# Group 0's scores at a later place, and the weighed probabilities of groups 1 and 2 turned by DVE and memory instead of TensorE

## The chip, the cores and the metric

The kernel runs on one core of a Trainium2 chip, as one launch. The metric is the device time of one execution in microseconds, and the profile is of one execution on the chip. Engines are named as the profile names them: PE is TensorE, DVE VectorE, ACT ScalarE, POOL GpSimd, SP the queue that loads weights; PEld is TensorE's loading of the stationary operand.

## What is computed

Two layers of a decoder over 512 tokens of width 1024, each a mixer and a gated MLP with a convolution of width 3. The change lies in the mixer of the second layer: three groups of dilated causal attention, four heads of width 128 each. Cut to what matters:

```python
DIL_PATTERNS = ((128, 1), (512, 4), (2048, 16))        # window, dilation

def odd_mixer(h, w_in, q_gain, k_gain, w_out):
    z = (h @ w_in).reshape(B, S, DIL_GROUPS, 3, DIL_HEADS, DIL_DH)
    q = rmsnorm(z[:, :, :, 0], q_gain)
    k = rmsnorm(z[:, :, :, 1], k_gain)
    v = z[:, :, :, 2]
    for g, (window, dilation) in enumerate(DIL_PATTERNS):
        o_g, lse_g = dilated_branch(q[:, :, g], k[:, :, g], v[:, :, g], dilation, window // dilation)
        ...
    wts = softmax(stack(lses), axis=0)                  # the groups' weights, by their denominators
    o = sum(wts[..., None] * stack(outs), axis=0)
    return o.reshape(B, S, ODD_MIX) @ w_out
```

`dilated_branch` is a causal softmax over the keys at distance 0, d, 2d, ... up to the window.

## The kernel before

The residual stream stands transposed in SBUF (`xT`: feature by token), and every projection runs in three matmuls on operands split into a high and a low part: hi x hi, hi x lo, lo x hi. Weights come from memory in slabs of 512 KB. For a slab `load_next` issues the load from SP, ScalarE rounds it to `hi` (L179), and DVE takes the rest to `lo` (L182). There are three buffers of each, and a slab is loaded two ahead of the one that TensorE reads.

TensorE's order is written by the program itself. `now` counts the microseconds of matmul work given to TensorE so far. `at(delay, fn, tag)` puts a function into a heap, to be called when `now` has come `delay` further, and `run` calls those that are due after each step of a projection (six matmuls in this layer). `drain(tag)` calls all that are left under a tag. So a delay is a place between projection matmuls, and no engine waits for a time. The order of the other engines' queues comes from a scheduler of the framework; each queue works strictly in order.

In the second layer's mixer the tokens stand by residue (token mod 4). `tok_gemm` gives one projection of 512 columns for all tokens: four tiles of 128 tokens, each in a PSUM bank of its own, four slabs, 96 matmuls (L333). The projections run in the order q and k of group 0, q and k of group 1, q and k of group 2, then the values of the three groups. A bank is a 128 x 512 tile of the pool `ps`, which has eight.

A finished q or k tile goes through `qk_evict`: ScalarE squares it (L367), DVE sums (L369), ScalarE and DVE form the reciprocal root (L213 to L218), DVE scales it out of the bank (`qn`, L401). Then it is transposed without TensorE. `turn` lets DVE transpose it in squares of 32 (L387, two buffers) and ScalarE's queue write these to memory (L389); `settle` reads them back in four parts from POOL's queue (L394); ScalarE copies the result into `q` or `k` (L416, L414). In group 0 each of these copies fills a part of every token tile, so its scores need all four tiles of q and k; in groups 1 and 2 a score needs the tile with its own number alone.

`scores(g, t, q, k)` takes one token tile: TensorE multiplies (L901 for group 0, two banks; L912 for groups 1 and 2, one bank), DVE adds the mask and takes the maximum while it moves the scores into `PR[g]` (L282), ScalarE exponentiates and sums (L891). The first score of a group is entered behind the last tile of k (`after_k`), each further one 5.0 us after the one before. Behind group 0's last score POOL moves its statistics to the order of the other groups through memory (`residues`). Behind group 2's last score `factors` forms one factor for each group, token and head, and sends group 0's back through memory (`e0`, `f0`, on POOL's queue).

Then `weigh(g, h)` is called twelve times, 10.0 + 3.5 i us later: DVE multiplies the blocks of `PR[g]` by their factor (L967: 7 blocks of 128 x 128 a head in group 0, 4 in groups 1 and 2), then TensorE transposes them (L974, up to four in a bank) and ScalarE brings the result back into `PR[g]` (L976). Groups 1 and 2 have 32 such transposes, group 0 has 28. At last `pv(h)` adds the products of values and probabilities of all three groups in one bank (L989, 15 products a head), and the output projection follows (L350).

The profile's line numbers are those of this kernel:

Of the kernel before, what the change touches and what calls it, by code (L numbers as in the profile page):

```python
# [129 lines left out]
def trunk_kernel(ctx: ExitStack, tc: tile.TileContext, x, weights, params, lqks, w_a2, consts, out):  # L130
# [740 lines left out]
    with tc.tile_pool(name="m1", bufs=1) as m1:  # L871
# [8 lines left out]

        PR = [m1.tile([P, 4, 7, P], F32, name="PR0")] + [m1.tile([P, 4, NT, P], F32, name=f"PR{g}") for g in (1, 2)]
        vts = [m1.tile([P, NT, 512], F32, name=f"vt{g}") for g in range(3)]
        fac = []

        def probs(dst, sc, g, t, h):

# [6 lines left out]
        def scores(g, t, q, k):  # L893
            ts = slice(t * P, (t + 1) * P)
            if g == 0:
                nk = P if t == 0 else 2 * P
                for hp in range(2):
                    sc = bank()
                    for h in range(2):
                        o = h * 256  # L900
                        T.matmul(sc[:, o:o + nk], q[:, 2 * hp + h, ts], k[:, 2 * hp + h, (t + 1) * P - nk:(t + 1) * P],  # L901
                                 start=(h == 0), stop=(h == 1))
                    pe(8 * nk * PASS)
                    for h in range(2):
                        b0 = max(0, 2 * t - 1)
                        dst = PR[0][:, 2 * hp + h, b0:b0 + nk // P].rearrange("p b k -> p (b k)")
                        probs(dst, sc[:, h * 256:h * 256 + nk], 0, t, 2 * hp + h)
            else:
                sc = bank()
                for h in range(4):  # L910
                    hs = slice(h * P, (h + 1) * P)
                    T.matmul(sc[:, hs], q[:, h, ts], k[:, h, ts], start=(h == 0), stop=(h == 3))  # L912
                pe(0.87)
                for h in range(4):
                    probs(PR[g][:, h, t], sc[:, h * P:(h + 1) * P], g, t, h)
            if t < NT - 1:
                at(5.0, lambda: scores(g, t + 1, q, k), "scores")
            elif g == 0:
                residues()
            elif g == 2:  # L920
                factors()
# [13 lines left out]
        def factors():  # L935
# [20 lines left out]
            for r in range(4):  # L956
                G.dma_start(f0[32 * r:32 * r + 32], e0.rearrange("(t l) r h -> r l t h", t=NT)[r])
            fac.extend((f0, eg[:, 1], eg[:, 2]))
            for i in range(12):
                at(10.0 + 3.5 * i, lambda i=i: weigh(i // 4, i % 4), "weigh")  # L960

        def weigh(g, h):

            nb = 7 if g == 0 else 4
            for b in range(nb):
                t = (b + 1) // 2 if g == 0 else b
                V.tensor_scalar(PR[g][:, h, b], PR[g][:, h, b], fac[g][:, t, h:h + 1], None, ALU.mult)  # L967

            def tr():
                for b0 in range(0, nb, 4):  # L970
                    n = min(4, nb - b0)
                    pt = bank()
                    for b in range(n):
                        T.transpose(pt[:, b * P:(b + 1) * P], PR[g][:, h, b0 + b], ident)  # L974
                    pe(0.107 * n)
                    A.activation(PR[g][:, h, b0:b0 + n].rearrange("p b k -> p (b k)"), pt[:, :n * P], AF.Copy)  # L976
            at(1.5, tr, "weigh")

        def pv(h):

# [4 lines left out]
            for i, (g, b) in enumerate(blocks):  # L985
                t, kb = ((b + 1) // 2, b // 2) if g == 0 else (b, b)
                to, w = (n0[:, t], PR[g][:, h, b].rearrange("p (r l) -> p r l", r=4)) if g == 0 else \
                    (n12[:, t], PR[g][:, h, b])
                T.matmul(to, vts[g][:, kb, h * P:(h + 1) * P], w, start=(i == 0), stop=(i == len(blocks) - 1))  # L989
            pe(0.218 * len(blocks))  # L990
            return po
# [1 line left out]
        def after_k(g, q, k):  # L993
            def f(t):
                if t == NT - 1:
                    at(2.5 if g == 0 else 1.0, lambda: scores(g, 0, q, k), "scores")
            return f

        def by_tile(dst, r):
# [52 lines left out]
```

## Time and profile before

| | |
|---|---|
| three timed runs | 1230.1, 1233.0, 1233.14 us (median 1233.0) |
| the profiled execution, its own time | 1230.4 us |
| its span in the trace | 1228.6 us |
| TensorE busy | 1215.2 us, 99% of the span |
| VectorE, ScalarE, GpSimd busy | 779.3, 546.6, 68.4 us |

The span is what the trace covers; the execution's own time has 1.8 us more around it. Times in a row are from the span's start. A matmul's length overlaps with the next one's, so work on TensorE is measured from start to start. The second layer's mixer lies between about 605 and 865 us.

### The profile page before, as it was taken

To read this page: it belongs to the slowest core of one execution; us is meant where nothing else is said; L and a number is where in the kernel's file an instruction comes from. 1 tells how busy PE (TensorE), PEld (TensorE's weight loads), DVE (VectorE), ACT (ScalarE), POOL (GpSimd) and SP (SyncE) were. 2 spreads that over 40 slices of the span, in tenths; PEclk is the share of its full clock that TensorE was granted. 3 is DMA by queue.
4 is the path that set the end of the run, shared out by engine and by line. 5 is a ranking of instruction groups with operands and counts; after the bars stand their busy time and mean duration, and the time that the engine had idled before them with its cause. 6 is when DMAs were issued, how large, how long until landed. Compare 5 with 4: busy or idle time off the path is not lost.

```text
span 1228.6 us, 15071 instructions
## 1 busy us (share of the span) xinstructions
PE 1215.2 (99%) x5687; PEld 1006.4 (82%) x5687; DVE 779.3 (63%) x1474; ACT 546.6 (44%) x896; POOL 68.4 (6%) x131
## 2 busy tenths in 40 slices
PE   9999999999999999999998999999999999999998
PEld 7888788788888888888886888889888888888887
DVE  7557868787753775366756676444877537763673
ACT  6446655454422443144534655544544314431441
POOL 0000000000000000000022324300000000000000
PEclk9999999999999999999999999999999999999999
DMA  7222111323323323332455456421233232332322
GB/s 256 87 87 70 49 56 38 100 88 102 103 86 103 99 91 103 94 91 71 137 159 169 123 162 203 140 87 51 88 103 95 94 103 93 96 103 88 101 77 95
DMA packets 41160, 127.14 MB, mean 103 GB/s; under 512 B 6359, under 2 KB 7288, under 8 KB 41088
## 3 DMA queue, kind: packets, MB, share of 16 engines
q1 hardware_dynamic: 32400, 110.38, 29.1%
q0 software_dynamic: 3936, 7.41, 2.3%
q10 hardware_dynamic: 4752, 8.39, 1.8%
q8 instruction: 44, 0.72, 0.2%
q14 instruction: 28, 0.23, 0.1%
HBM read 116.70 MB, written 8.41 MB: 102 GB/s over the span
## 4 chain that ended last, share of the span: by engine, by line
PE 95%; DMA 2%; DVE 1%; POOL 1%; ACT 0%; issue 0%; SPq 0%; POOLq 0%; ACTq 0%; DVEq 0%
PE bank L766 39%; PE bank L333 22%; PE bank L808 20%; PE bank L350 7%; DMA z<-turned 1%; PE bank L989 1%; PE bank L536 1%; PE bank L570 1%; DMA turned<-turn 1%; PE bank L901 1%; PE bank L912 1%; PE bank L379 1%; POOL z L394 1%; PE bank L974 1%; PE bank L558 0%; PE bank L664 0%
## 5 line engine op out<-in xcount | busy, mean ns | idle before, releaser
L179 ACT ACTIVATE hi<-raw 128x1024 fp32r<-128x1024 f32 (+2 forms) x209 | 217.0, 1039 | 280.7 <-PE bank L808 143.2
L182 DVE TENSOR_TENSOR lo<-raw,hi 128x1024 fp32r<-128x1024 f32 (+2 forms) x209 | 250.5, 1199 | 128.8 <-ACT hi L179 120.1
L766 PE MATMUL bank<-hhi,hi 128*128 128x512 f32 x704 | 273.9, 389 | 0.0
L766 PE MATMUL bank<-hhi,lo 128*128 128x512 f32 x704 | 273.9, 389 | 0.0
L766 PE MATMUL bank<-hlo,hi 128*128 128x512 f32 x704 | 273.9, 389 | 0.0
L333 PE MATMUL bank<-hi,hhi 128*128 128x512 f32 (+2 forms) x480 | 185.2, 386 | 0.5 <-ACT hi L179 0.5
L333 PE MATMUL bank<-lo,hhi 128*128 128x512 f32 (+2 forms) x480 | 181.1, 377 | 0.2 <-DVE lo L182 0.2
L333 PE MATMUL bank<-hi,hlo 128*128 128x512 f32 (+2 forms) x480 | 180.5, 376 | 0.0
L766 PEld LDWEIGHTS bank<-hhi,hi 128*128 128x128 f32 x704 | 132.2, 188 | 27.5
L766 PEld LDWEIGHTS bank<-hhi,lo 128*128 128x128 f32 x704 | 132.2, 188 | 27.4
L766 PEld LDWEIGHTS bank<-hlo,hi 128*128 128x128 f32 x704 | 132.2, 188 | 27.3
L808 PE MATMUL bank<-ghi,lo 128*128 128x512 f32 (+1 forms) x358 | 138.0, 385 | 0.0
L808 PE MATMUL bank<-glo,hi 128*128 128x512 f32 (+1 forms) x358 | 138.0, 385 | 0.0
L808 PE MATMUL bank<-ghi,hi 128*128 128x512 f32 (+1 forms) x358 | 138.0, 385 | 0.0
L333 PEld LDWEIGHTS bank<-lo,hhi 128*128 128x128 f32 x480 | 90.4, 188 | 17.7 <-DVE lo L182 1.0
L333 PEld LDWEIGHTS bank<-hi,hhi 128*128 128x128 f32 x480 | 90.6, 189 | 17.1 <-ACT hi L179 1.0
L333 PEld LDWEIGHTS bank<-hi,hlo 128*128 128x128 f32 x480 | 90.7, 189 | 15.4
L813 DVE TENSOR_TENSOR xT<-xT,bank 128x512 f32<-128x512 f32 (+1 forms) x49 | 33.0, 675 | 106.4 <-PE bank L808 106.2
L394 POOL DMA_DIRECT2D z<-turned x96 | 52.0, 549 | 514.0 <-DVE rs_a L213 435.9
L808 PEld LDWEIGHTS bank<-ghi,hi 128*128 128x128 f32 x358 | 67.2, 188 | 13.6
L808 PEld LDWEIGHTS bank<-glo,hi 128*128 128x128 f32 x358 | 67.2, 188 | 13.5
L808 PEld LDWEIGHTS bank<-ghi,lo 128*128 128x128 f32 x358 | 67.3, 188 | 13.5
(203 smaller groups left out, 1358.7 us busy)
## 6 DMA issues: line engine op xcount, KB each, us to landing
raw<-in_weights_dram SPq DMA_DIRECT2D x189, 512.0 KB, 3.5
raw<-in_weights_dram SPq DMA_DIRECT2D x16, 384.0 KB, 3.1
turned<-turn ACTq DMA_DIRECT2D x24, 256.0 KB, 2.9
z<-turned POOLq DMA_DIRECT2D x96, 64.0 KB, 3.8
xT<-in_xT_dram SPq DMA_DIRECT2D x7, 256.0 KB, 5.8
out_dram<-xT ACTq DMA_DIRECT2D x7, 256.0 KB, 2.0
raw<-in_weights_dram SPq DMA_DIRECT2D x2, 544.0 KB, 3.5
vt<-vs POOLq DMA_DIRECT2D x16, 64.0 KB, 2.2
```

What stands on the lines that cost most here:

```text
L179: r = A.activation(hi[:, c0:c1], raw[:, c0:c1], AF.Copy)
L182: V.tensor_tensor(out=lo[:, c0:c1], in0=raw[:, c0:c1], in1=hi.bitcast(F32)[:, c0:c1], op=ALU.subtract)
L333: T.matmul(ps[t][:, :n], lhs(a[:, kc], t), b[:, k, :n], start=(kc == 0 and j == 0), stop=(kc == DC - 1 and j == 2))
L350: T.matmul(ps, w[:, k, d * P:(d + 1) * P], r(k), start=(k == 0 and j == 0), stop=(k == nk - 1 and j == 2))
L379: T.transpose(pt[:, h * P:(h + 1) * P], src[:, h * P:(h + 1) * P], ident)
L394: G.dma_start(to[32 * j:32 * j + 32].rearrange("c i b r -> c i (b r)"), d[j])
L536: T.matmul(sc[:, :nk], qT[rs, h, n * P:(n + 1) * P], kT[rs, h, :nk], start=True, stop=True)
L570: T.matmul(po[n][:, h * P:(h + 1) * P], wT[:, j * P:(j + 1) * P], bv[:, j, h * P:(h + 1) * P], start=(h == 0 and j == 0), stop=(h == 3 and ...
L766: T.matmul(ps, w[:, kc], r[:, kc], start=(kc == 0 and m == 0), stop=(kc == DC - 1 and m == 2))
L808: T.matmul(ps[:, ts], a[:, k], b[f0 + k][:, ts], start=(k == 0 and m == 0), stop=(k == n - 1 and m == 2))
L813: V.tensor_tensor(out=xT[:, c, ts], in0=xT[:, c, ts], in1=ps[:, ts], op=ALU.add)
L901: T.matmul(sc[:, o:o + nk], q[:, 2 * hp + h, ts], k[:, 2 * hp + h, (t + 1) * P - nk:(t + 1) * P], start=(h == 0), stop=(h == 1))
```

## The change

Four places. Group 0's first score is entered 10.5 us after its k is complete, and not 2.5. Group 2's scores are entered 4.0 us apart, and not 5.0. The eight calls of `weigh` for groups 1 and 2 come first, from 1.0 us after `factors` on, 2.5 apart, the two groups in turn; the four for group 0 come at 12.0 + 4.0 h, and their transposes 3.0 after that. For groups 1 and 2 `weigh` no longer calls TensorE: the weighed blocks of a head go through `turn` and `settle`, as q and k do, back into the same `PR[g]`, and `pv` reads block b there as four runs of 32 columns, which stand 128 numbers apart.

```diff
@@ -880,7 +880,7 @@
 
         PR = [m1.tile([P, 4, 7, P], F32, name="PR0")] + [m1.tile([P, 4, NT, P], F32, name=f"PR{g}") for g in (1, 2)]
         vts = [m1.tile([P, NT, 512], F32, name=f"vt{g}") for g in range(3)]
-        fac = []
+        fac, turned = [], {}
 
         def probs(dst, sc, g, t, h):
 
@@ -914,7 +914,7 @@
                 for h in range(4):
                     probs(PR[g][:, h, t], sc[:, h * P:(h + 1) * P], g, t, h)
             if t < NT - 1:
-                at(5.0, lambda: scores(g, t + 1, q, k), "scores")
+                at(5.0 if g < 2 else 4.0, lambda: scores(g, t + 1, q, k), "scores")
             elif g == 0:
                 residues()
             elif g == 2:
@@ -956,8 +956,10 @@
             for r in range(4):
                 G.dma_start(f0[32 * r:32 * r + 32], e0.rearrange("(t l) r h -> r l t h", t=NT)[r])
             fac.extend((f0, eg[:, 1], eg[:, 2]))
-            for i in range(12):
-                at(10.0 + 3.5 * i, lambda i=i: weigh(i // 4, i % 4), "weigh")
+            for i in range(8):
+                at(1.0 + 2.5 * i, lambda i=i: weigh(1 + i % 2, i // 2), "weigh")
+            for h in range(4):
+                at(12.0 + 4.0 * h, lambda h=h: weigh(0, h), "weigh")
 
         def weigh(g, h):
 
@@ -965,6 +967,12 @@
             for b in range(nb):
                 t = (b + 1) // 2 if g == 0 else b
                 V.tensor_scalar(PR[g][:, h, b], PR[g][:, h, b], fac[g][:, t, h:h + 1], None, ALU.mult)
+
+            if g > 0:
+                w = PR[g][:, h].rearrange("p b k -> p (b k)")
+                turned[g, h] = w.rearrange("p (i b l) -> p i b l", i=4, b=NT)
+                settle(turned[g, h], turn(m1, w, NT))
+                return
 
             def tr():
                 for b0 in range(0, nb, 4):
@@ -974,7 +982,7 @@
                         T.transpose(pt[:, b * P:(b + 1) * P], PR[g][:, h, b0 + b], ident)
                     pe(0.107 * n)
                     A.activation(PR[g][:, h, b0:b0 + n].rearrange("p b k -> p (b k)"), pt[:, :n * P], AF.Copy)
-            at(1.5, tr, "weigh")
+            at(3.0, tr, "weigh")
 
         def pv(h):
 
@@ -985,7 +993,7 @@
             for i, (g, b) in enumerate(blocks):
                 t, kb = ((b + 1) // 2, b // 2) if g == 0 else (b, b)
                 to, w = (n0[:, t], PR[g][:, h, b].rearrange("p (r l) -> p r l", r=4)) if g == 0 else \
-                    (n12[:, t], PR[g][:, h, b])
+                    (n12[:, t].rearrange("p (i l) -> p i l", i=4), turned[g, h][:, :, b])
                 T.matmul(to, vts[g][:, kb, h * P:(h + 1) * P], w, start=(i == 0), stop=(i == len(blocks) - 1))
             pe(0.218 * len(blocks))
             return po
@@ -993,7 +1001,7 @@
         def after_k(g, q, k):
             def f(t):
                 if t == NT - 1:
-                    at(2.5 if g == 0 else 1.0, lambda: scores(g, 0, q, k), "scores")
+                    at(10.5 if g == 0 else 1.0, lambda: scores(g, 0, q, k), "scores")
             return f
 
         def by_tile(dst, r):
```

How it moves the queues, at three places. **ScalarE where group 0's k is completed.** `sq`, `rs_y` and `hi` are of group 1's q and of the weight slabs; L414 is a tile of group 0's k, L891 is the exponential of a score of group 0. Before:

```order
L414 ACTIVATE k<-z 128x16x32
L367 ACTIVATE sq<-bank,rstd_5160 128x512
L214 ACTIVATE rs_y_5678<-rs_a_5677 128x4
L215 ACTIVATE rs_y_5678<-rs_y_5678 128x4
L414 ACTIVATE k<-z 128x16x32
L389 DMA turned_5692<-turn 128x512
L891 ACTIVATE PR_5073,st_5069<-PR_5073,st_5069 128x128 x4
L367 ACTIVATE sq<-bank,rstd_5160 128x512 x2
L179 ACTIVATE hi<-raw 128x1024
```

Now:

```order
L414 ACTIVATE k<-z 128x16x32
L367 ACTIVATE sq<-bank,rstd_5160 128x512 x2
L214 ACTIVATE rs_y_5678<-rs_a_5677 128x4
L215 ACTIVATE rs_y_5678<-rs_y_5678 128x4
L414 ACTIVATE k<-z 128x16x32
L214 ACTIVATE rs_y_5710<-rs_a_5709 128x4
L367 ACTIVATE sq<-bank,rstd_5160 128x512
L215 ACTIVATE rs_y_5710<-rs_y_5710 128x4
L179 ACTIVATE hi<-raw 128x1024
L367 ACTIVATE sq<-bank,rstd_5160 128x512
L389 DMA turned_5692<-turn 128x512
```

The four exponentials of the first score stood right behind the write that follows k's last tile; now squares and roots of group 1's q and a weight slab stand there, and one more square stands ahead of that tile. On TensorE the first score (L901) has moved 42 projection matmuls back: 264 stand between the last L252 and it, where there were 222. The scores of group 1 begin 12 projection matmuls earlier than before, and those of group 2 stand where they did, 24 matmuls apart.

**DVE from the factors on.** `PR_5073` is group 0, `PR_5074` group 1, `PR_5075` group 2. Before:

```order
L953 TENSOR_TENSOR eg<-eg,den 128x16 x3
L967 TENSOR_SCALAR PR_5074<-PR_5074,eg 128x128 x10
L182 TENSOR_TENSOR lo<-raw,hi 128x1024
L967 TENSOR_SCALAR PR_5074<-PR_5074,eg 128x128 x6
L967 TENSOR_SCALAR PR_5075<-PR_5075,eg 128x128 x11
L967 TENSOR_SCALAR PR_5073<-PR_5073,f_5080 128x128 x7
L182 TENSOR_TENSOR lo<-raw,hi 128x1024
L967 TENSOR_SCALAR PR_5073<-PR_5073,f_5080 128x128 x21
L967 TENSOR_SCALAR PR_5075<-PR_5075,eg 128x128 x5
```

Now:

```order
L953 TENSOR_TENSOR eg<-eg,den 128x16 x3
L969 TENSOR_SCALAR PR_5074<-PR_5074,eg 128x128 x4
L969 TENSOR_SCALAR PR_5075<-PR_5075,eg 128x128
L387 STREAM_TRANSPOSE turn<-PR_5074 128x4x4x32
L969 TENSOR_SCALAR PR_5075<-PR_5075,eg 128x128 x3
L182 TENSOR_TENSOR lo<-raw,hi 128x1024
L387 STREAM_TRANSPOSE turn<-PR_5075 128x4x4x32
L969 TENSOR_SCALAR PR_5074<-PR_5074,eg 128x128 x4
L969 TENSOR_SCALAR PR_5075<-PR_5075,eg 128x128
L387 STREAM_TRANSPOSE turn<-PR_5074 128x4x4x32
L969 TENSOR_SCALAR PR_5075<-PR_5075,eg 128x128 x3
L969 TENSOR_SCALAR PR_5074<-PR_5074,eg 128x128 x4
```

The weighings of groups 1 and 2 are now broken up by transposes in squares of 32, and those of group 0 begin between them; they go on in this way for 20 rows more.

**TensorE at the end of the value projection.** L974 are transposes, L989 (now L997) the products. Before:

```order
L974 MATMUL bank<-cst,PR_5074 128x128 x4
L974 MATMUL bank<-cst,PR_5075 128x128 x16
L989 MATMUL bank<-PR_5073,vt_5076 128x4x32 x7
L989 MATMUL bank<-PR_5074,vt_5077 128x128 x4
L989 MATMUL bank<-PR_5075,vt_5078 128x128 x4
```

Now:

```order
L333 MATMUL bank<-hi,hhi 128x512
L333 MATMUL bank<-hi,hlo 128x512
L333 MATMUL bank<-lo,hhi 128x512
L997 MATMUL bank<-PR_5073,vt_5076 128x4x32 x7
L997 MATMUL bank<-PR_5074,vt_5077 128x128 x4
L997 MATMUL bank<-PR_5075,vt_5078 128x128 x4
```

The twenty transposes ahead of the products are gone, and the last projection matmuls stand there; the remaining transposes of group 0, seven a head, come 78, 96, 102 and 120 matmuls behind group 2's last score, 24 ahead of the products. On ScalarE's queue eight writes of squares come in and eight evictions go; on POOL's queue eight times four readings come in behind those of `f`.

## Rows read from the trace of the kernel before

**Rows 1.** The page, part 1: busy time of each engine, its share of the span, and its instructions.

```profile
PE 1215.2 (99%) x5687; PEld 1006.4 (82%) x5687; DVE 779.3 (63%) x1474; ACT 546.6 (44%) x896; POOL 68.4 (6%) x131
```

**Rows 2.** What TensorE waited for in the whole span: waiting engine and line, what released it, us in total, times, longest us.

```profile
PE bank L901 <- ACT k L414: 5.8, 1, 5.8
PE bank L224 <- DVE hhi L221: 1.5, 1, 1.5
PE bank L350 <- ACT oahi L206: 1.3, 1, 1.3
```

**Rows 3.** TensorE's timeline around group 0's first score: start us, length us, engine, line, operation, output and input, count, and in brackets the idle time before it and what ended it. L333 are the projection's matmuls, L901 are group 0's scores (eight records for one query tile).

```profile
667.15 0.39 PE L333 MATMUL bank<-lo,hhi 128*128 128x512 f32 x1
673.35 2.08 PE L901 MATMUL bank<-k,q 128*128 128x128 f32 x8 [5.81 <-ACT k L414]
675.08 0.77 PE L333 MATMUL bank<-hi,hhi 128*128 128x512 f32 x1
...
681.54 1.89 PE L901 MATMUL bank<-k,q 128*128 128x256 f32 x8
```

**Rows 4.** Busy time of each engine in stretches of the span, with TensorE's granted clock (PEclk, 1.00 is full speed), the share of the DMA engines and GB/s. The first stretch lies behind a stop of 1.28 us that ends at 222.18, the others are the stop before group 0's first score and what follows it.

```profile
222.20:226.00 3.80, 3.19 (x13) 2.33 (x14) 1.27 (x2) 0.00 (x0) 0.00 (x0) 1.00 0.45 138
667.50:673.30 5.80, 0.04 (x1) 0.00 (x0) 4.84 (x10) 3.18 (x7) 1.32 (x3) 0.73 0.69 214
673.30:675.10 1.80, 1.75 (x9) 1.75 (x9) 0.59 (x5) 0.15 (x1) 0.00 (x0) 0.50 0.48 184
675.10:677.00 1.90, 1.90 (x7) 1.51 (x7) 0.53 (x6) 1.58 (x8) 0.97 (x2) 0.51 0.00 0
```

**Rows 5.** TensorE's timeline around a score of group 2 (L912, eight records as in group 0's first), columns as in rows 3.

```profile
783.32 1.05 PE L912 MATMUL bank<-k,q 128*128 128x128 f32 x8
784.12 0.48 PE L333 MATMUL bank<-hi,hhi 128*128 128x512 f32 x1
...
789.66 1.05 PE L912 MATMUL bank<-k,q 128*128 128x128 f32 x8
```

**Rows 6.** ScalarE's timeline while TensorE stands, columns as in rows 3: the square of group 1's first q tile (L367), the first step of its reciprocal root (L214), and the last copy into group 0's `k` (L414).

```profile
668.98 0.67 ACT L367 ACTIVATE sq<-bank,rstd 128x512 f32<-128x512 f32 x1
670.64 0.20 ACT L214 ACTIVATE rs_y<-rs_a 128x4 f32<-128x4 f32 x1 [1.00 <-DVE rs_a L213]
...
672.67 0.63 ACT L414 ACTIVATE k<-z 128x512 f32<-128x512 f32 x1 [1.58 <-DMA z<-turned]
```

**Rows 7.** ScalarE's timeline at the end of the value projection: the split of a weight slab (`hi`, L179), and the eviction of the last value tile (`vt`, L424).

```profile
827.85 1.06 ACT L179 ACTIVATE hi<-raw 128x1024 fp32r<-128x1024 f32 x1 [0.42 <-PE bank L333]
828.81 0.67 ACT L424 ACTIVATE vt<-bank,rstd 128x512 f32<-128x512 f32 x1
```

**Rows 8.** VectorE's timeline while TensorE stands, on group 1's first q tile: sum of squares (L369), scaling (`qn`, L401), transpose in squares of 32 (`turn`, L387).

```profile
669.72 0.68 DVE L369 TENSOR_REDUCE ss<-sq 128x4 f32<-128x512 f32 x1
...
671.97 0.69 DVE L401 TENSOR_TENSOR qn<-bank,rr 128x512 f32<-128x512 f32 x1
672.70 0.71 DVE L387 STREAM_TRANSPOSE turn<-qn 128x512 f32<-128x512 f32 x1
```

**Rows 9.** VectorE's timeline where the probabilities are weighed (L967; `eg` holds the factors of groups 1 and 2, `f` those of group 0), with the splits of weight slabs between (`lo`, L182).

```profile
795.52 2.05 DVE L967 TENSOR_SCALAR PR<-PR,eg 128x128 f32<-128x128 f32 x10
797.50 1.22 DVE L182 TENSOR_TENSOR lo<-raw,hi 128x1024 fp32r<-128x1024 f32 x1
798.63 3.42 DVE L967 TENSOR_SCALAR PR<-PR,eg 128x128 f32<-128x128 f32 x17
803.06 1.47 DVE L967 TENSOR_SCALAR PR<-PR,f 128x128 f32<-128x128 f32 x7 [1.01 <-DMA f<-e]
...
805.57 4.21 DVE L967 TENSOR_SCALAR PR<-PR,f 128x128 f32<-128x128 f32 x21
```

**Rows 10.** ScalarE's timeline: the copy of the first k tile of group 1.

```profile
716.44 0.63 ACT L414 ACTIVATE k<-z 128x512 f32<-128x512 f32 x1 [2.51 <-DMA turned<-turn]
```

**Rows 11.** TensorE's timeline: the first score of group 1.

```profile
723.48 1.05 PE L912 MATMUL bank<-k,q 128*128 128x128 f32 x8
```

**Rows 12.** TensorE's timeline at the end of the value projection: transposes of weighed probabilities (L974), the products with the values (L989), the output projection (L350).

```profile
816.11 0.93 PE L974 MATMUL bank<-cst,PR 128*128 128x128 f32 x7
...
819.65 0.60 PE L974 MATMUL bank<-cst,PR 128*128 128x128 f32 x4
...
827.88 2.35 PE L974 MATMUL bank<-cst,PR 128*128 128x128 f32 x20
830.06 13.56 PE L989 MATMUL bank<-PR,vt 128*128 128x128 f32 x120
843.38 0.48 PE L350 MATMUL bank<-o1hi,hi 128*128 128x512 f32 x1
```

**Rows 13.** The writes of turned squares to memory, issued from ScalarE's queue (L389, 256 KB each, 24 in the span): time from issue to landing.

```profile
DMA to landing us min/median/max: 2.0/2.9/5.0
```

**Rows 14.** Their readings back, issued from POOL's queue (L394, 64 KB each): what POOL spends to issue one, in ns, and the time from issue to landing.

```profile
L394 POOL DMA_DIRECT2D z<-turned x96: 548/548/562, 632.3 to 771.0; - x96
...
DMA to landing us min/median/max: 2.1/3.8/5.6
```

**Rows 15.** The products of probabilities and values, by line: duration of a record, smallest, median and largest, in ns. 56 of the 120 records are of group 0 and write with a permuted shape (4 x 32), 64 are of groups 1 and 2.

```profile
L989 PE MATMUL bank<-PR,vt x120: 275/275/275, 830.1 to 843.4; 128*128 128x128 f32 x120
```

**Rows 16.** POOL's timeline: the issue of the four readings of `f`.

```profile
797.93 2.19 POOL L957 DMA_DIRECT2D f<-e  x4 [1.41 <-DMA e<-eg]
```

## The prediction

> **What bounds the kernel now.** I read the busy shares first: TensorE is busy for 1215.2 us, 99% of the span [rows 1]. The time is TensorE's work plus its stops, and another engine counts only where TensorE waits for it. The list of what TensorE waited for comes next: one stop of 5.8 us for `k` of group 0, written by ScalarE at L414, then nothing above 1.5 us [rows 2]. TensorE's timeline at that stop shows a second price: the last matmul before it begins at 667.15, so the next could have begun at 667.38; the scores begin at 673.35, and for some 3.5 us everything is slow [rows 3]. The windows say why: the granted clock averages 0.73 in the stop, then reads 0.50 and 0.51 (1.2 GHz) until 677, after TensorE had done nothing for 5.8 us; behind a stop of 1.28 us at 222.18 it reads 1.00 [rows 4].
>
> **Group 0's scores enter later.** What the stop costs, by comparison with a score of group 1 or 2, which has the same eight records at full clock: there 0.80 us from the score's start to the next projection matmul, and 5.54 us for the 24 matmuls behind it [rows 5]. Here the start is 673.35 - 667.38 = 5.97 us late, the score takes 1.73 instead of 0.80, and the 24 matmuls take 6.46 instead of 5.54 [rows 3]. Sum: 5.97 + 0.93 + 0.92 = **7.8 us**.
>
> By the built order the first score now stands 42 projection matmuls later. At 5.54/24 = 0.23 us each [rows 5] TensorE reaches it at 667.4 + 9.6 = 677.0. `k`'s last tile is begun at 672.67 and takes 0.63 [rows 6]: ready at 673.3, 3.7 us to spare. All that makes `k` was issued before the stop, so this arrival is unchanged.
>
> A smaller wait takes its place. At the new position group 1's k projection has begun, so its four PSUM banks and the four of group 1's q take all eight. The score's two banks must be those of q's tiles 0 and 1, which DVE has to have read (`qn`, L401). ScalarE's queue holds them back: `k`'s last tile now stands ahead of what q's tiles 1 to 3 need. From 673.2 on it runs L214 (0.20), a square (0.67), L215 (0.2), a `hi` (1.05, L179 [rows 7]) and a square (0.67) [rows 6]: until 676.0. DVE then does a sum (0.68), some small steps (about 1 us) and `qn` of tile 1 (0.69) [rows 8]: 678.4. The second half of the score, due at 677.0 + 0.4, waits **1.0 us**. Bounds: 0 if the queues run ahead of this count; 3 us if DVE's `lo` (1.22 [rows 9]) and square transpose (0.71 [rows 8]) come in series too, and then 1.85 us for the clock, in all 4.9. I take 1.0, nearer to the 1.28 us stop that left the clock alone [rows 4].
>
> Group 1's scores move as well: 12 matmuls (2.7 us) earlier, with group 0's last score (1.5 us) now ahead of them, so 1.2 us net. Before, k's tile 0 was ready at 716.44 + 0.63 [rows 10] for a score at 723.48 [rows 11], 6.4 us early. DVE now takes tile 1's sum and small steps ahead of tile 0, about 2 us. Some 3 us are left: cost nothing. If that cover went, it would be a stop like the one removed. Group 0's statistics go through the POOL queue behind group 1's k instead of ahead; their reader stands on DVE behind group 1's last score, tens of us later: nothing. The delay of 4.0 instead of 5.0 for group 2 changes nothing: 24 matmuls stand between its scores in both orders.
>
> **Groups 1 and 2 off TensorE.** 32 of the 60 transposes go. From 819.65, where the first of them begins, to 830.06, where the products start, there are 10.41 us [rows 12], of which 30 projection matmuls take 30 x 0.227 = 6.80. So the transposes cost **3.6 us**, all on the path. Eight ScalarE evictions go too, off the path. The last 20 transposes also covered the eviction of the last value tile: `vt` follows ScalarE's last `hi` at 828.81, 0.67 long [rows 7], 1.83 us after TensorE's last projection matmul began. Without them the products start 0.23 us after that matmul, but the tile is read by the fifteenth of them (14 x 0.222 = 3.1 us [rows 12]): 1.5 us to spare, nothing.
>
> What comes in is off TensorE: eight square transposes on DVE at 0.71 [rows 8], eight writes from ScalarE's queue landing in 2.0 to 5.0 us [rows 13], 32 reads on POOL's at 0.55 us each to issue [rows 14]. POOL needs 32 x 0.55 = 17.6 us from about 800, and the last lands 3.8 (at most 5.6) later, near 823; the products start at about 826 on this clock and group 2's last head is read 12 us into them. Hidden.
>
> The products read groups 1 and 2 as four runs of 32 with a gap. No row has such a reading; the nearest is that products of group 0, which write with that shape, and the others all take 275 ns [rows 15]. Bounds: 0, and doubled (32 x 0.222 = 7.1 us). I take 0, as the shape of the writing cost nothing.
>
> Group 0's 28 transposes stay and come 18, 6 and 18 matmuls apart, and must not overtake DVE. DVE's queue from 795.52, by 0.20 us for a weighing (17 in 3.42) and 1.14 for a `lo` [rows 9], with 0.62 to 0.71 for a square transpose, and the wait for `f` until 803.06 [rows 9], gives heads 0, 1 and 2 ready at 806.9, 812.2 and 815.0. TensorE (790.5 + 78 x 0.227, then 0.81 for seven transposes, from 819.65 - 816.11 less 12 matmuls [rows 12]) is there at 808.2, 813.1 and 815.2. Head 2 has no room: **0.2 us**, with bounds 0 and 3.8 (3 x 1.2 us more by the count under C, every write at the slowest landing, 5.0).
>
> The Trainium skill has a rule against leaving so much to these queues: GPSIMD Engine Reference, Key points, says that GpSimd shares its SBUF interfaces with VectorE and that they contend. If DVE stood still while POOL issues, the last weighings would come up to 17 us later. The rows disagree for the issuing of DMAs: with POOL issuing from 797.93 to 800.1 [rows 16] the weighings run at 0.20, and alone at 4.21/21 = 0.20 [rows 9].
>
> **Sum** against the profiled execution's own 1230.4 us (a span of 1228.6 and 1.8 around it): 1230.4 - 7.8 + 1.0 - 3.6 + 0.2 = **1220.2**. The three timed runs are 1230.1, 1233.0 and 1233.14; the profiled one belongs to the faster kind, 2.6 below the median. As nothing in the trace says what makes that difference, I take the middle between 1220.2 and 1222.8: **1221.5**.
>
> **Rivals.** (A) The waits come back: score and head 2 at their upper bounds, 4.9 and 3.8 us, give 1220.2 + 3.9 + 3.6 = 1227.7, a half of that 1224 to 1225. For it: both margins are under 1.5 us. Against: the chain of `qn` is counted from measured steps. (B) Strided reading doubles the 32 products: 1227.3. (C) The round trip blocks DVE, and the kernel is slower. DVE has two buffers for squares, so its third to eighth transpose each wait for the write of two before. With a landing time L the eighth ends near 797 + 3 x (L + 0.9) + 3 us. Up to L = 3.8 DVE's own work sets the pace; from there each us of L costs 3 on head 2's transposes, and with a stop over 5 us the clock's 1.85. The 11.4 us of both gains less the 1.2 of waits are gone at L near 7 us, and with L = 9 the time is 1230.4 - 10.2 + 15.6 + 1.85 = 1237.6. Against it: the slowest of 24 such writes took 5.0 us [rows 13]. The Trainium skill sides with this rival: VectorE: DVE Perf Modes, The three transpose paths, calls a plain copy that does the transposing by its access pattern 19 times slower than the crossbar's. By that rule (C) would hold; the trace disagrees for these copies, whose runs are 128 numbers long. (D) The change doesn't remove the stop: the weight loads beside it delay `k` by 3.7 us or more and the wait only moves; then just the transposes are gained, 1226.8.
>
> **How the numbers follow.** Chances: the forecast (1217.5 to 1225) 0.78, A 0.10, B 0.04, C 0.04, D 0.04. The range leaves out C, the worst of A and a little below: 1217.5 to 1228. A measurement of this kernel can tell about 0.3%, 3.7 us, from no change. Against each run's own kind, faster by more than that are the forecast and half of A, 0.83; within it half of A, B, D and a quarter of C, 0.14; slower three quarters of C, 0.03.
>
> **What would show it.** Right: TensorE's list of waits without `k` at L414, in its place about 1 us for DVE's `qn` at the first score, and a clock of 1.00 around it; 28 transposes at 0.81 us a head; products that start without a wait and take 13.3 us. Wrong: a stop at the first score over 3 us (A or D), products of groups 1 and 2 over 275 ns (B), writes that land after 7 us and TensorE waiting for DVE's weighings (C), or TensorE waiting for a read of POOL's.

## The result and the profile after

| | before | now |
|---|---|---|
| four timed runs, median (range) | 1232.16 us (1230.1 to 1233.14) | 1224.19 us (1221.89 to 1224.99) |
| profiled execution, its span | 1228.6 us | 1220.1 us |
| stretch A | 173.54 us | 166.77 us |
| stretch B | 52.91 us | 50.54 us |

The ratio is 0.9935, with a 95% interval of 0.9924 to 0.9947: 8.0 us faster. Two stretches of TensorE's timeline carry the comparison. A runs from the first projection matmul behind the last L252 (616.93 before, 617.52 now) to the first one behind group 2's last score (790.47 and 784.29). B runs from there to the output projection's first matmul (843.38 [rows 12] and 834.83). A gave 6.77 us and B 2.37. The span shrank by 8.5 and not by 9.1, since TensorE began A 0.59 us later in this execution, for reasons ahead of the change.

What TensorE waits for now, the first three of its list (waiting line, what released it, us in total, times, longest):

```profile
PE bank L224 <- DVE hhi L221: 1.5, 1, 1.5
PE bank L350 <- ACT oahi L206: 1.3, 1, 1.3
PE bank L901 <- DVE qn L401: 0.7, 1, 0.7
```

The 5.8 us for `k` [rows 2] are gone, and a wait for `qn` stands in their place, as forecast. TensorE's timeline there, start and length first:

```profile
677.49 0.60 PE L901 MATMUL bank<-k,q 128*128 128x128 f32 x4
678.84 0.71 PE L901 MATMUL bank<-k,q 128*128 128x128 f32 x4 [0.74 <-DVE qn L401]
```

and VectorE's, with the `qn` that it waits for:

```profile
675.95 1.22 DVE L182 TENSOR_TENSOR lo<-raw,hi 128x1024 fp32r<-128x1024 f32 x1
...
678.10 0.68 DVE L401 TENSOR_TENSOR qn<-bank,rr 128x512 f32<-128x512 f32 x1
```

The score's second half was due 0.40 behind its first (half of the 0.80 of [rows 5]), at 677.89, and came 0.95 us late. The clock stays whole around it (stretch, busy times, then PEclk, DMA share, GB/s):

```profile
677.50:681.00 3.50, 2.76 (x16) 2.27 (x15) 3.50 (x13) 1.41 (x3) 2.17 (x4) 1.00 0.68 193
```

In B the products are as fast as before [rows 15], though 64 of the 120 records now read four runs of 32:

```profile
L997 PE MATMUL bank<-PR,vt x120: 270/275/275, 821.5 to 834.8; 128*128 128x128 f32 x120
```

What B lost against the forecast stands in group 0's transposes, TensorE's timeline again:

```profile
802.07 0.93 PE L982 MATMUL bank<-cst,PR 128*128 128x128 f32 x7
...
806.94 1.62 PE L982 MATMUL bank<-cst,PR 128*128 128x128 f32 x7
...
809.79 1.52 PE L982 MATMUL bank<-cst,PR 128*128 128x128 f32 x7
```

The first set takes 0.68 us from its start to the next matmul, the second 1.38 and the third 1.28, without a long stop: the transposes come at the pace of DVE's weighings. 1.3 us are lost, where 0.2 were expected. VectorE's timeline says why:

```profile
803.97 1.22 DVE L182 TENSOR_TENSOR lo<-raw,hi 128x1024 fp32r<-128x1024 f32 x1
806.32 0.71 DVE L387 STREAM_TRANSPOSE turn<-PR 128x512 f32<-128x512 f32 x1 [1.13 <-DMA turned<-turn]
806.96 1.23 DVE L969 TENSOR_SCALAR PR<-PR,f 128x128 f32<-128x128 f32 x6
```

The seventh square transpose stands ahead of six weighings of head 1 and waits 1.13 us for its buffer, that is for the write of the fifth. It is the only one of the eight that waits. ScalarE's queue issued that write at 801.17, and the line's view for this write alone gives its landing time:

```profile
DMA to landing us min/median/max: 4.7/4.7/4.7
```

### The profile page after: what moved, and what is told of

It reads as the page before. It is cut to its first block, busy times and chain, and to the rows that moved or that the text cites. A ratio compares the mean times of both kernels' runs of the same rounds, so it can differ in the third digit from the quotient of the medians.

```text
span 1220.1 us, 15087 instructions
## 1 busy us (share of the span) xinstructions
PE 1211.4 (99%) x5655; PEld 1002.0 (82%) x5655; DVE 783.2 (64%) x1482; ACT 540.7 (44%) x888; POOL 86.0 (7%) x163
## 4 chain that ended last, share of the span: by engine, by line
PE 96%; DMA 1%; DVE 1%; ACT 1%; issue 0%; POOL 0%; SPq 0%; POOLq 0%; DVEq 0%
PE bank L766 39%; PE bank L333 22%; PE bank L808 20%; PE bank L350 7%; PE bank L997 1%; PE bank L536 1%; PE bank L570 1%; DMA z<-turned 1%; PE bank L912 1%; PE bank L379 1%; DVE lo L182 0%; PE bank L901 0%; PE bank L558 0%; PE bank L664 0%; DMA xT<-in_xT_dram 0%; PE bank L698 0%
## 5 line engine op out<-in xcount | busy, mean ns | idle before, releaser
L179 ACT ACTIVATE hi<-raw 128x1024 fp32r<-128x1024 f32 (+2 forms) x209 | 216.9, 1039 | 283.9 <-PE bank L808 143.2
L182 DVE TENSOR_TENSOR lo<-raw,hi 128x1024 fp32r<-128x1024 f32 (+2 forms) x209 | 250.6, 1199 | 126.7 <-ACT hi L179 117.3
L333 PE MATMUL bank<-hi,hhi 128*128 128x512 f32 (+2 forms) x480 | 184.3, 384 | 0.4 <-ACT hhi L206 0.4
L333 PE MATMUL bank<-lo,hhi 128*128 128x512 f32 (+2 forms) x480 | 180.8, 377 | 0.6 <-DVE lo L182 0.6
L333 PE MATMUL bank<-hi,hlo 128*128 128x512 f32 (+2 forms) x480 | 180.3, 376 | 0.0
L333 PEld LDWEIGHTS bank<-lo,hhi 128*128 128x128 f32 x480 | 90.2, 188 | 17.8 <-DVE lo L182 1.4
L333 PEld LDWEIGHTS bank<-hi,hhi 128*128 128x128 f32 x480 | 90.5, 188 | 17.1 <-ACT hhi L206 0.8
L333 PEld LDWEIGHTS bank<-hi,hlo 128*128 128x128 f32 x480 | 90.4, 188 | 15.6 <-DVE hlo L207 0.2
L394 POOL DMA_DIRECT2D z<-turned x96 | 52.0, 549 | 515.6 <-DVE rs_a L213 435.8
```

What stands on the lines that cost most here:

```text
L179: r = A.activation(hi[:, c0:c1], raw[:, c0:c1], AF.Copy)
L182: V.tensor_tensor(out=lo[:, c0:c1], in0=raw[:, c0:c1], in1=hi.bitcast(F32)[:, c0:c1], op=ALU.subtract)
L333: T.matmul(ps[t][:, :n], lhs(a[:, kc], t), b[:, k, :n], start=(kc == 0 and j == 0), stop=(kc == DC - 1 and j == 2))
L394: G.dma_start(to[32 * j:32 * j + 32].rearrange("c i b r -> c i (b r)"), d[j])
```

## The experiments

A and B are of each kernel's one profiled execution, the ratio is to the kernel before, of several timed runs. The changed kernel and e7, which run the same instructions in the same order, differ by 1.0 us in A and 0.3 in B, so smaller differences between two profiles prove nothing by themselves.

| kernel | A us | B us | ratio (95% interval) |
|---|---|---|---|
| before | 173.54 | 52.91 | 1 |
| changed | 166.77 | 50.54 | 0.9935 (0.9924 to 0.9947) |
| e1 later score alone | 167.99 | 52.91 | 0.9952 (0.9937 to 0.9967) |
| e2 turning alone | 174.40 | 50.77 | 0.9983 (0.9975 to 0.9992) |
| e3 score at 13.0 | 165.73 | 51.38 | 0.9924 (0.9912 to 0.9936) |
| e4 five buffers | 166.23 | 49.25 | 0.9922 (0.9911 to 0.9934) |
| e5 score at 4.5 | 172.41 | 51.24 | 0.9954 (0.9935 to 0.9973) |
| e7 still two buffers | 167.75 | 50.85 | 0.9935 (0.9916 to 0.9954) |
| e9 both mends | 165.73 | 49.27 | 0.9910 (0.9896 to 0.9925) |
| e10 two heads more | 165.74 | 47.94 | 0.9892 (0.9878 to 0.9907) |
| e11 one buffer | 166.98 | 51.04 | 0.9925 (0.9909 to 0.9942) |
| e12 all heads | 166.24 | 56.37 | 0.9965 (0.9953 to 0.9977) |

**e1, the later score alone.** In the kernel before:

```diff
-                    at(2.5 if g == 0 else 1.0, lambda: scores(g, 0, q, k), "scores")
+                    at(10.5 if g == 0 else 1.0, lambda: scores(g, 0, q, k), "scores")
```

> The kernel before with one edit: group 0's first score 10.5 behind its k. Two stretches of TensorE's timeline are compared. A: from the first projection matmul behind the last L252 to the first one behind group 2's last score (before 616.93 to 790.47, 173.54 us; changed kernel 617.52 to 784.29, 166.77). B: from there to the output projection's first matmul (52.91 and 50.54). Theory, the two parts of the change add up: A 166.8 with a clock of 1.00 and a wait of about 1 us for qn, B 52.9, time 6.8 below before, 1225.4 (ratio 0.9945). Rival, the change's whole gain is the stop and the transposes gave nothing beyond the difference of one run from another: the ratio is that of the changed kernel, 0.9935. Rival, the stop only moves: A 172 or more, 1230 or more.

The ratio is 5.9 us of gain, with an interval that holds the 6.8. TensorE's list of waits names `qn` again, for longer, and a second wait at group 1's first score:

```profile
PE bank L901 <- DVE qn L401: 1.2, 1, 1.2
...
PE bank L912 <- ACT k L414: 0.5, 1, 0.5
```

So the stop is gone and only small waits follow it. Group 1's cover, put at some 3 us, was thin: here its k is half a microsecond late, and in the changed kernel it was ready 0.7 us ahead.

**e2, the turning alone.** In the changed kernel:

```diff
-                    at(10.5 if g == 0 else 1.0, lambda: scores(g, 0, q, k), "scores")
+                    at(2.5 if g == 0 else 1.0, lambda: scores(g, 0, q, k), "scores")
```

> The changed kernel with group 0's first score back at 2.5. Theory, the parts add up and the second one gives what its own stretch showed: A 173.5 with the stop of 5.8 us at the first score and a clock of 0.50 behind it, B 50.5, time 2.4 below before, 1229.8 (ratio 0.9981). Rival, the late weighings in B came from the later scores: B 49.5, 3.4 below before, 1228.8. Rival, the transposes were hidden anyway: B 52.9, 1232.2.

The first theory's numbers: B 50.77 and 0.9983. The late weighings are there without the later scores. A is 0.9 longer than expected, nearly all of it by the clock (last section). The gains of e1 and e2 add up within their intervals: 0.0048 + 0.0017 = 0.0065 of the time, the changed kernel's own.

**e3, the score another 12 matmuls later.** In the changed kernel `at(10.5 ...)` becomes `at(13.0 ...)`.

> The changed kernel with group 0's first score at 13.0, 12 matmuls further back. Theory, what is left at that score is the wait for qn of tile 1 alone, ready at 678.8 when TensorE came at 677.9; 12 matmuls (2.7 us) later TensorE doesn't wait: A 165.8, time 0.95 below the changed kernel, 1223.2 (ratio 0.9928). Rival, the next link of DVE's and ScalarE's queues is as late and the wait moves to a later score or to a bank of the projection: A 166.8 or more, 1224.2.

A is 165.73, as expected: the wait for `qn` is gone from TensorE's list and nothing takes its place in A. B was 0.8 longer than in the changed kernel's profile, on the same rows (the second and third set of transposes): the fifth square's write landed 5.6 us after its issue there, and DVE's seventh transpose waited 1.7.

**e4, five buffers.** In the changed kernel:

```diff
-    def turn(pool, src, n):
+    def turn(pool, src, n, name="turn", bufs=2):
-        sq = pool.tile([P, 4, 4, 32], F32, name="turn", bufs=2)[:, :, :n]
+        sq = pool.tile([P, 4, 4, 32], F32, name=name, bufs=bufs)[:, :, :n]
...
-                settle(turned[g, h], turn(m1, w, NT))
+                settle(turned[g, h], turn(m1, w, NT, *(("z", 3) if g == 2 else ("turn", 2))))
```

> The changed kernel with five buffers for the weighed squares in place of two (group 2's go into the three z tiles, which are idle by then). In the changed kernel two of group 0's sets of seven transposes took 1.38 and 1.28 us instead of 0.68, waiting for DVE's weighings, 1.3 us in all. Theory 1, DVE was held by its seventh square transpose, which waited 1.13 us for the write of the fifth out of the same buffer: without that wait the weighings come 1.1 us earlier, the sets cost about 1.0 less, B 49.5, time 1223.2 (ratio 0.9927). Theory 2, DVE's own work is what is late (eight transposes, sixty weighings and the weight slabs' splits in one queue): B 50.4 to 50.5, 1224.2.

B is 49.25, theory 1. All four sets of transposes take 0.68 or 0.69, on TensorE's timeline:

```profile
808.03 0.93 PE L982 MATMUL bank<-cst,PR 128*128 128x128 f32 x7
...
810.17 0.93 PE L982 MATMUL bank<-cst,PR 128*128 128x128 f32 x7
```

DVE does the same work in nearly the same order, and the seventh square transpose no longer waits, so it was the wait for the buffer and not DVE's load.

**e5, the score at 4.5.** In the changed kernel `at(10.5 ...)` becomes `at(4.5 ...)`.

> The changed kernel with group 0's first score at 4.5, 12 matmuls behind its place in the kernel before and 30 ahead of its place in the changed one. TensorE comes there 53.1 us into stretch A (see the runs before), and k is ready at 56.2: a stop of 3.1 us. Theory 1, what a stop costs is its length and, where the clock falls, 1.85 us more; here it falls, as behind the 5.8 us: A 165.8 + 3.1 + 1.85 = 170.8, time near 1228. Theory 2, a stop of that length leaves the clock at 1.00: A 168.9, time near 1226. Rival to both, k comes later because fewer matmuls have gone by, so the stop stays at 5.8: A 173.5, time near 1231.

None of the three sums fits. The rival's is nearest (173.5), but its mechanism isn't there: the stop is 3.5 us and not 5.8, so `k` doesn't come later for want of matmuls ahead of it. Theory 1's mechanism is there, and A is 1.6 longer than it said. TensorE's timeline and the windows behind the stop (columns as above):

```profile
674.37 2.08 PE L901 MATMUL bank<-k,q 128*128 128x128 f32 x8 [3.50 <-ACT k L414]
```

```profile
674.00:678.00 4.00, 3.63 (x13) 3.25 (x14) 2.94 (x16) 1.08 (x4) 0.00 (x0) 0.50 0.13 50
678.00:682.00 4.00, 4.00 (x14) 3.16 (x13) 2.52 (x9) 3.36 (x12) 0.80 (x2) 0.69 0.35 131
```

The stop is 0.4 longer than the 3.1 expected (`k`'s last copy begins 56.15 us behind the start of A, 55.59 in the changed kernel), and the slow clock lasts further: the score takes 1.73 instead of 0.80 and the next 24 matmuls 7.63 instead of 5.54 [rows 5], 3.0 us where the kernel before paid 1.85.

**e7, one buffer, which it wasn't.** In the changed kernel a tile is taken ahead of each turn:

```diff
+                m1.tile([P, 4, 4, 32], F32, name="turn", bufs=2)
                 settle(turned[g, h], turn(m1, w, NT))
```

> The changed kernel with one buffer for the weighed squares in place of two (a second one is taken and left idle at each turn). Theory (rival C of the prediction, made true): each square transpose waits for the write before it, some 0.4 to issue and 3.1 to 5 to land, so one comes every 4.3 us or so, and the seventh and eighth stand ahead of group 0's weighings of heads 1 and 2 on DVE: TensorE stops some 10 us in group 0's transposes, its clock falls, B 60 to 64, time 1234 to 1238, slower than before. Rival, the scheduler puts group 0's weighings ahead of the late transposes, so that DVE's waits cost little: B 50 to 53, time 1224 to 1227.

The edit failed: the idle tile was given back at once, and both buffers stayed in use (the second square transpose begins at 794.86, 1.6 us after the first one's write is issued, and doesn't wait; no write of these squares landed in under 2.0). What was run is the changed kernel once more: on TensorE, VectorE, ScalarE and GpSimd its trace has the same instructions in the same order. So it shows how far one order varies from one execution to the next. B is 50.85, and `qn` makes the score's second half 1.90 us late in place of 0.95:

```profile
681.02 0.71 PE L901 MATMUL bank<-k,q 128*128 128x128 f32 x4 [1.70 <-DVE qn L401]
```

**e9, both mends:** the edits of e3 and e4 together.

> The changed kernel with both mends: first score at 13.0 and five buffers. Theory, the two waits were independent: A 165.7, B 49.3, time 1231.8 - 7.8 - 3.6 = 1220.4 (ratio 0.9907), no wait of TensorE over 0.3 us in either stretch. Rival, one mend brings the other's wait back (the later scores press on DVE where the probabilities are weighed, as the later score alone showed 51.4 in B): B 50.5 or more, 1221.7 or more.

A 165.73 and B 49.27: the two waits were independent. The whole list of waits has nothing of A or B left (the four lie elsewhere in the span):

```profile
PE bank L224 <- DVE hhi L221: 1.5, 1, 1.5
PE bank L350 <- ACT oahi L206: 1.3, 1, 1.3
PE bank L350 <- DVE oalo L207: 0.6, 1, 0.6
PE bank L333 <- DVE lo L182: 0.4, 1, 0.4
```

**e10, heads 2 and 3 of group 0 as well.** On top of e9, in `weigh`, with `pv` reading the blocks in `turned`:

```diff
+            if g == 0 and h > 1:
+                for b0, n in ((0, 4), (4, 3)):
+                    w = PR[0][:, h, b0:b0 + n].rearrange("p b k -> p (b k)")
+                    z = w.rearrange("p (i b l) -> p i b l", i=4, b=n)
+                    turned.update({(0, h, b0 + b): z[:, :, b] for b in range(n)})
+                    settle(z, turn(m1, w, n))
+                return
```

> The kernel with both mends, and heads 2 and 3 of group 0 turned by DVE and memory too (14 of TensorE's last 28 transposes go, in four more square transposes, four writes and sixteen reads). Theory, a transpose on TensorE's path costs 0.097 us and nothing that comes in is waited for: B 49.3 - 1.4 = 47.9, time 1219.0 (ratio 0.9896). Rival, POOL's queue is full by now: 48 reads at 0.55 us, the last issued near 825 and landing near 829, where head 3's products stand at 830; products wait up to 3 us, B 49 to 51, time 1220 to 1222.

B is 47.94. The 14 transposes were worth 1.33 us, 0.095 each, and no product waits. With 0.9892 this is the fastest kernel of the study, and its interval (0.9878 to 0.9907) lies clear of the changed kernel's. POOL's last read is issued near the end of its cover: it lands 2.1 us later, at 827.2, and head 3's products begin at about 827.5.

```profile
825.14 0.55 POOL L394 DMA_DIRECT2D PR<-turned  x1 [0.41 <-DMA PR<-turned]
```

**e11, one tile for all eight squares.** In the changed kernel `turn` is handed one `z` tile, taken in `factors`:

```diff
+            one.append(m1.tile([P, 4, 4, 32], F32, name="z", bufs=3))
...
-                settle(turned[g, h], turn(m1, w, NT))
+                settle(turned[g, h], turn(m1, w, NT, one[0]))
```

> The changed kernel with one tile for all eight weighed squares, so that each square transpose waits for the write before it (the second try, since in the first the idle buffer was given back at once and two were in use). The built order of DVE puts six weighings of head 0 ahead of the third transpose, head 1's ahead of the fifth, heads 2 and 3 behind the fifth. Theory (rival C's mechanism, at its price of one landing for each transpose): one transpose comes every 4.3 to 4.8 us from 790, the fifth at 807 to 809, and head 2's weighings stand 2.1 behind it: TensorE, there at 809.1 by the changed kernel's clock, stops for some 1 to 2 us, and the last two sets of squares come back near 830, when head 3's products start at about 832: B 50.5 to 53, time 1224 to 1227, no gain from the second part. Rival 1, the landing time rises as well, above 7 us: B 60 or more, 1234 or more. Rival 2, DVE's waits are covered: B 49.3 as with five buffers.

B is 51.04, in the theory's range, but TensorE waited elsewhere. All sets of transposes take 0.68. VectorE's last square waits for the write before it, and ScalarE's queue (ACTq rows are issues of writes) shows that square's write with the value tiles behind it:

```profile
822.02 0.71 DVE L387 STREAM_TRANSPOSE z<-PR 128x512 f32<-128x512 f32 x1 [3.87 <-DMA turned<-z]
...
822.76 0.33 ACTq L389 DMA_DIRECT2D turned<-z  x1
823.13 0.98 ACT L985 ACTIVATE PR<-bank 128x512 f32<-128x512 f32 x2 [3.44 <-PE bank L333]
824.00 1.85 ACT L424 ACTIVATE vt<-bank,rstd 128x512 f32<-128x512 f32 x3
...
826.65 0.72 ACT L424 ACTIVATE vt<-bank,rstd 128x512 f32<-128x512 f32 x1
```

The write waits for its square, which DVE ended at 822.7, and the evictions queue behind it. TensorE's products stop for the last one:

```profile
827.42 2.83 PE L998 MATMUL bank<-PR,vt 128*128 128x128 f32 x23 [1.03 <-ACT vt L424]
```

**e12, all heads of group 0.** On top of e10 the condition becomes `if g == 0:` and the products take the groups in the order 1, 2, 0.

> The kernel with both mends, and all four heads of group 0 turned by DVE and memory too (no transpose of probabilities is left on TensorE; the products take groups 1 and 2 first, group 0 last). Theory, POOL's queue is the next bound: with heads 2 and 3 it issued its last read at 825.1, 48 reads in all; with 64 the last is issued near 834 and lands near 838, where TensorE wants head 3's squares at about 828: a stop of some 9 us and the clock falls behind it, B 46.6 + 9 + 2 = 57 to 58, time near 1229. Rival, the queue takes them in earlier because POOL stood idle for 8 us between reads: B 46.6 to 48, time 1218 or less.

The size came out near (B 56.37), the cause was another. TensorE's products stop three times for value tiles, not for reads:

```profile
820.65 0.49 PE L1005 MATMUL bank<-PR,vt 128*128 128x128 f32 x2 [1.76 <-ACT vt L424]
825.02 0.79 PE L1005 MATMUL bank<-PR,vt 128*128 128x128 f32 x2 [3.88 <-ACT vt L424]
826.82 14.89 PE L1005 MATMUL bank<-PR,vt 128*128 128x128 f32 x108 [1.00 <-ACT vt L424]
```

The longest has the same picture as in e11: DVE's square waits for its buffer, ScalarE's write for the square, and a value tile stands behind the write.

```profile
823.16 0.71 DVE L387 STREAM_TRANSPOSE turn<-PR 128x512 f32<-128x512 f32 x1 [3.51 <-DMA turned<-turn]
...
823.91 0.33 ACTq L389 DMA_DIRECT2D turned<-turn  x1
824.28 0.69 ACT L424 ACTIVATE vt<-bank,rstd 128x512 f32<-128x512 f32 x1 [3.68 <-DVE turn L387]
```

The clock reads 0.50 from 825 to 830. POOL issues its last read at 836.7, so it may have been the next to be late; with the evictions in front of it, that isn't shown.

## Why the prediction was right, and where it was off

The time lies in the range, the way is the forecast's, and 1221.5 was 2.7 us too low.

**The stop (7.8 us).** Right. e1 and e2 split the two parts, and without any wait left (e3, e9) A is 165.73, 7.81 below before.

**The wait for `qn` (1.0 us).** Right in its mechanism, with luck in how near the size came. In the five profiles with the score at 10.5 it is 0.41 (e4), 0.95 (changed kernel), 1.16 (e11), 1.41 (e1) and 1.90 (e7). `k`'s last copy begins 55.05, 55.59, 55.81, 56.06 and 56.55 us behind the start of A in them: what `k` is late, `qn` is late, through ScalarE's queue, as the prediction has it. ScalarE's timeline in the changed kernel and in e7 (starts of A 617.52 and 618.75):

```profile
673.11 0.64 ACT L414 ACTIVATE k<-z 128x512 f32<-128x512 f32 x1 [1.21 <-DMA z<-turned]
```

```profile
675.30 0.63 ACT L414 ACTIVATE k<-z 128x512 f32<-128x512 f32 x1 [1.32 <-DMA z<-turned]
```

The copy waits for `k`'s readings to land, and that moment, which the prediction took from one execution, sets the size. e3 took the wait away for 1.04. The `lo` that was left to the upper bound did come in series, and some of the small steps ran ahead instead.

**Group 1's scores (nothing, some 3 us of cover).** The price held, the cover did not: 0.7 us in the changed kernel, and 0.5 us of stop in e1.

**The 32 transposes (3.6 us).** Right, by B without waits (e9): 52.91 - 49.27 = 3.64. The four-run reading cost nothing, against rival B.

**Head 2's transposes (0.2 us, bounds 0 and 3.8).** This is the term that was mis-sized. The mechanism was in the prediction, under C: from a landing time of 3.8 us on, the two buffers and no longer DVE's work set the pace. It was then priced as if writes landed faster than that, though the slowest of [rows 13] took 5.0. In the changed kernel one took 4.7, DVE's seventh transpose waited, and heads 1 and 2 lost 1.3 us. In the five profiles with two buffers one transpose waits, once, and the loss (B above 49.27) goes with the landing of the fifth square's write: 1.3 to 1.6 us where it took 4.7, 2.0 and 2.1 where it took 5.2 and 5.6. e4 took just this away. The upper bound was too dear in turn, as it let three late landings come in series. The half of rival A that was put at 1224 to 1225 has the median's number and not its cause: 1.1 us of it came true, the rest of the way to 1224.19 is told under the step to the median.

**The round trip (hidden).** Right for the changed kernel: TensorE waits for no read, and the writes of weighed squares landed in 2.0 to 4.7 us. The Trainium skill's sentence on plain copies that transpose by strides (VectorE: DVE Perf Modes, The three transpose paths) is for copies whose innermost stride at the destination is large. The prediction leaves this condition out, and these copies, which move runs of 128 numbers, don't meet it; no run here has the crossbar's copy to compare. Nor did POOL hold up DVE: with POOL issuing reads from 806.44 to 811.05 and again from 811.47, eleven weighings from 809.70 on took 2.21 us, 0.20 each as in [rows 9]. `lo`, which reads two tiles, took 1.22 us at 799.30, with POOL issuing from 797.39 to 804.97, and 1.23 at 784.54, with POOL idle. The Trainium skill (GPSIMD Engine Reference, Key points) puts the contention on VectorE's instructions in a 2-port mode or with two inputs in SBUF; no trace here shows it for POOL's issuing of DMAs.

**Rival C (slower from a landing time near 7 us).** Its condition never came about: no write of a weighed square took 7 us (4.7 at most in the changed kernel, 6.5 in e4, whose five buffers hid it), so its price there is untested; from 4.7 to 5.6 us a later landing cost about its own lateness, where C counted three times as much. e11 made the transposes wait in another way, each for the write before it. DVE waited 7.8 us for writes and TensorE lost 1.8, in an order that C didn't have: the built one moved group 0's weighings ahead of the late transposes. What gave way first, there and in e12, was ScalarE's queue, for which the prediction had no price: a write that waits for its square holds the value tiles behind it. The Trainium skill has the rule (TensorE: Matmul & The Clock Gate, Architectural detail): ScalarE's and VectorE's queues are strictly first in, first out. The trace agrees, with stops of 1.03 us in e11 and up to 3.88 in e12.

**From 1230.4 to a median.** The 2.7 us have three parts. In the profiled stretches the sum was 10.2 and came to 9.1; A began 0.6 later in the execution; and the step from the profiled execution to the median, taken as half of 2.6 us for want of a cause, came to 2.3, 1.0 more. A likely cause of this step is in the last section.

## What to carry to other kernels

When a queue of other work stands behind an instruction that waits for a reused buffer, price one late landing, not the median and not every landing at its slowest; more buffers, here taken from tiles that were idle, are the cheap cure. A DMA issued from a compute engine's queue costs its issue only as long as its data are ready when it comes up: otherwise all that stands behind it waits too. Moving work off a TensorE that is 99% busy paid its start-to-start time (3.64 us where 3.6 were counted, and 1.33 where 1.4 were), until the queues that took it over ran out of slack. And a wait that hangs on a landing is a range: the same order gave 0.95 us and 1.90.

## What was not expected of the hardware

The clock's price for a stop isn't fixed. In the first layer, whose program is the same in all twelve kernels, TensorE stops at the same place for 1.28 us and then for 0.61 (before: stops that end at 222.18 and 223.53; [rows 4] has the first). In five of the twelve profiled executions the clock stays at 1.00 there, in seven it falls to 0.50 for a while. The changed kernel, and then e4, where the fall comes inside the window, so that its mean reads 0.61 (PEclk is the third number from the end):

```profile
224.00:226.00 2.00, 1.89 (x8) 1.59 (x9) 0.06 (x1) 0.00 (x0) 0.00 (x0) 1.00 0.80 199
```

```profile
224.00:226.00 2.00, 1.88 (x5) 1.55 (x6) 0.06 (x1) 0.00 (x0) 0.00 (x0) 0.61 0.71 215
```

From that stop to the start of A the first five take 394.75 or 394.76 us and the other seven 396.34 to 396.39: the fall costs 1.6 us, and it either happens or doesn't. It is likely a part of what sets one execution of the same kernel apart from another: the changed kernel's profiled execution, which was spared the fall, took 1221.89 us at a mean clock of 1.000, its other three 1223.68 to 1224.99 at 0.998 to 0.999. Where their clock fell isn't shown. The prediction read the clock of 1.00 behind this stop as a property of its length, and that was one execution's luck. The price of a long stop varies as well: 1.85 us in the kernel before, 2.6 in e2, 3.0 in e5, after stops of 5.8, 5.9 and 3.5 us. What decides it isn't shown.
